# Norm factors spread from their two columns, lambda worked out in the first mixer, and a tail by groups in seven transfers

## The chip, the cores and the metric

One Trainium2 chip, one core of it. The metric is the device time of one execution in microseconds; the median of three runs stands for a kernel. Where a profile is read, it is one further execution taken by the hardware profiler, with its own time.

## The reference

One inference step of a two-layer diffusion backbone, for 128 context tokens and 128 latent tokens of width 2048, in float32. In short:

```
for l in range(2):
    mod = silu(cond) @ w_ada[l] + b_ada[l]          # six vectors: shift, scale, gate, twice
    h = rmsnorm(x, g_norm_mix[l]) * (1 + sc1) + sh1
    x = x + gt1 * (mixer_ab(h) if l == 0 else mixer_c(h))
    h = rmsnorm(x, g_norm_ffn[l]) * (1 + sc2) + sh2
    x = x + gt2 * conv_ffn(h)                       # up 2048 -> 2 x 5632, conv of 3, silu gate, down
y = rmsnorm(x, g_final)
rmsnorm(x, g) = x * rsqrt(mean(x * x) + EPS) * g    # over a token's 2048 features
mixer_c: softmax(q1 k1) - lam * softmax(q2 k2), then v, a norm per head, * (1 - lambda_init), w_out
         lam = exp(sum(lq1 * lk1)) - exp(sum(lq2 * lk2)) + lambda_init
```

The context tokens use their own condition vector and attend to themselves; the latent tokens attend to themselves and to 128 cached keys. `mixer_ab` has eight heads of latent attention and eight of grouped-query attention. The outputs are y of both groups and the new cache tensors.

## The kernel before, in words

**Layout.** Features stand on the 128 partitions, tokens on the free dimension: x is a tile of 16 chunks (`KD`) of 128 features by 256 tokens (`NT`), the context tokens first (`T` = 128 each). The tokens of the two requests are the two groups g = 0, 1, which have modulation vectors of their own.

**Products.** Each float32 product is made of three on split operands: a weight tile is loaded raw (1 MB), ACT rounds it to a high half `wh` (line 244), DVE subtracts to get the low half `wl` (line 245), and `gemm` (lines 330 to 348) multiplies wh by the operand's high and low halves and wl by its high half. A product of one output chunk is 16 steps k of three such matmuls. `between` hooks run inside the steps; where a hook is given, the order on TensorE is kept as written (`keep_order`).

**Order.** The program is recorded through a tile framework whose scheduler simulates the engines and puts the instructions of each engine in an order of its own; each engine then executes its list in order. `keep_order` pins instructions against each other, and `pe.in_turn` does so for TensorE in some stages. A change of one instruction can thus move many others in the stages that aren't pinned, the first mixer's heads above all. Work for adaLN (the product of silu(cond) with w_ada, 96 MB) is spread over all stages by rates: `pump` (line 568) is called after each product and does as many steps of it as its rate has made due; `side_pump` and `side_step` do the "side" blocks on DVE (lines 482 to 526, tiles `aacc`, `block`, `amside`), at the rates of `SIDE` (line 83), and `side_flush` does what is left at the end of a stage.

**Norms.** `stat_add` squares a finished chunk of x on ACT and POOL adds it to `sqacc`; the last square stays apart. `stat_rstd` (line 220) sums over the partitions with four matmuls of one column, DVE adds EPS (`rv`, line 208), POOL takes the power -1/2 (`rr`, line 211). The result is a column for each group: tokens on the partitions, one number each. `diagonal` (line 228) turns these into two 128x128 diagonal matrices on DVE, and `spread` (line 235) multiplies a matrix of ones with them, so that every partition holds the factors of all 256 tokens in PSUM. This is done at the start, for the latents and keys of the first mixer, at three entries, and at the end.

**Entries.** At the FFN of layer 0, the mixer of layer 1 and its FFN, `modulated` (line 673) hides the norm: the first three output chunks are multiplied with unnormalised rows `u` and scaled afterwards (`scaled`), while the normalised, modulated rows are made for the rest: `row` (line 735), sixteen times, on DVE (x by the factor, 737; low half, 749), ACT (743; cast, 747) and POOL (745, 749). The hooks stand in line 710: in chunk 0, step 8, the statistic and the diagonal (`stats`); in chunk 1, step 2, the spread (`factor`); line 713: in chunk 1, step 11, the first adaLN sums (`sums(0)`), which also start two loads. Line 720 copies the factors to SBUF on ACT.

**Layer 1's mixer** (`mixer_c`, line 1093) begins with lambda: a product of two columns on DVE, one matmul with ones, an exponential on ACT (line 1101), a combination on DVE (`nlam`). Then `project(h)` makes q, k and v of each of eight heads: the first head's first three products are the ready ones of `modulated`. `rope` (line 771) rotates q and k, four DVE operations each. `attend` follows in pieces between later products.

**Tail.** The last FFN's down projection ends with chunk 15: `residual` (line 761) on DVE, its square on ACT, `norm_scale`, a copy of the factors on ACT (line 1351), and then 16 chunks of the output: five (`EARLY`) that already carry g_final on POOL, eleven on DVE (line 1357), sent in five transfers by `SENT` (lines 58, 1359).

Of the kernel before, what the change touches and what calls it, by code (L numbers as in the profile page):

```python
# [12 lines left out]
AF = mybir.ActivationFunctionType  # L13
# [44 lines left out]
SENT = (4, 8, 12, 14, 16)  # L58
# [24 lines left out]
SIDE = {"in3": 0.6, "heads": 1.05, "out0": 0.9, "c": 1.7, "outc": 0.7}  # L83
# [5 lines left out]
def step_kernel(ctx: ExitStack, tc: tile.TileContext, A: dict):  # L89
# [138 lines left out]
    def diagonal(r, cols):  # L228
        dg = T_(tmp, [P, 2 * T], "diag", bufs=1)
        for i, c in enumerate(cols):  # L230
            dve.tensor_scalar(out=dg[:, i * T:(i + 1) * T], in0=ident, scalar1=r[:, c:c + 1],
                              scalar2=None, op0=ALU.mult)
        return dg

    def spread(dg, cols=(0, 1), bank=bank):

        ps = bank()
        n = len(cols) * T
        pe.matmul(ps[:, :n], ones, dg[:, :n], start=True, stop=True)
        return ps[:, :n]  # L240
# [354 lines left out]
    def norm_scale(st):  # L595
        return spread(diagonal(stat_rstd(st, D), (0, 1)))
# [76 lines left out]
    def modulated(st, l, which, W, u, to, rp):  # L673


        ensure(l, 3 * which + 1)
        ensure(l, 3 * which)
        while later:
            later.pop(0)()
        for q in range(4):  # L680
            raw_shift(u, l, which, q)
        if which:
            ada["i"] += len(BESIDE[l])
        unit = ROWS[ada["i"]]
        raws, got = [], {}

        def load_tile():
            raw = T_(wpool, [P, 4, 512], "araw", bufs=2)
            sp.dma_start(out=raw, in_=A["w_ada"][unit[0], unit[1], unit[2], len(raws)])
            raws.append(raw)  # L690

        def stats():
            got["r"] = stat_rstd(st, D, att_bank)
            got["dg"] = diagonal(got["r"], (0, 1))

        def factor():
            got["rb"] = spread(got["dg"], bank=att_bank)

        def sums(t):
            for i in range(2):  # L700
                sum_rows(t + i, raws[t + i])
            if t == 0:
                load_tile()
                load_tile()
            else:
                ada["i"] += 1
                steps.extend(ada_finish(*unit, False))
                steps.pop(0)()
# [11 lines left out]
        act.copy(rbs, rb)  # L720
# [12 lines left out]
        return hx, ready, [(lambda: steps.pop(0)(keep_order))] if steps else []  # L733
# [17 lines left out]
    def scaled(p, rb):  # L751
# [7 lines left out]
        return t  # L759

# [73 lines left out]
    def mixer_ab(hx, rb0, beside):  # L834
        l = 0
        with tc.tile_pool(name="ab", bufs=1) as ab:
            with tc.tile_pool(name="abp", bufs=1) as pj:
# [39 lines left out]
                def latents(c):  # L877
                    stat_add(sk, ck[:, c], 4)
                    if c == 3:
# [4 lines left out]
                        dg = diagonal(r, (0, 1))  # L884
                        yield
                        rb = spread(dg)
# [15 lines left out]
                def keys(c):  # L902
# [4 lines left out]
                    for g in range(2):  # L907
# [4 lines left out]
                    dg = diagonal(r, (0, 1))  # L912
                    yield
                    dve.scalar_tensor_tensor(out=kb[:, c], in0=kb[:, c], scalar=C("gkn"),
                                             in1=spread(dg), op0=ALU.mult, op1=ALU.mult)
# [84 lines left out]
            with tc.tile_pool(name="abh", bufs=1) as hp:  # L1000
# [33 lines left out]
                flush()  # L1034
                start(gqa_query(0))
# [57 lines left out]
    def mixer_c(cp, hx, W, ready, st):  # L1093
        l = 1
        lm = T_(cp, [P, 2], "lm")
# [4 lines left out]
        ex = T_(cp, [P, 2], "ex")  # L1100
        act.activation(ex, ps[:, 0:2], AF.Exp)
        nlam = T_(cp, [P, 1], "nlam")
        dve.scalar_tensor_tensor(out=nlam, in0=ex[:, 1:2], scalar=-LAMBDA_INIT, in1=ex[:, 0:1],
                                 op0=ALU.add, op1=ALU.subtract)

        xh, xl = (lambda k: hx[:, k, :NT]), (lambda k: hx[:, k, NT:2 * NT])
# [12 lines left out]
        def project(h):  # L1119
# [8 lines left out]
            if h == 1:  # L1128
                side_start("c", BESIDE[1], cp, True)
            for dst, to in ((q, T), (k, 2 * T)):  # L1130
# [5 lines left out]
                rope(dst[:, :, to:], ev[:, :, T:], 2, 64, "rch", "rsh")  # L1136
# [8 lines left out]
        def attend(h, q, k, v, evs):  # L1145
# [40 lines left out]
            for g in range(2):  # L1186
# [48 lines left out]
    def ffn(hx, W, ready, turn, l, st):  # L1235
# [4 lines left out]
        with tc.tile_pool(name=f"ffn{l}", bufs=1) as fp, banks(f"pffn{l}") as pf:  # L1240
# [41 lines left out]
            def down(gs, q):  # L1282
# [4 lines left out]
                for c in range(KD):  # L1287
# [5 lines left out]
                    residual(ps, l, 1, c, st if q == NQ - 1 else None)  # L1293
# [55 lines left out]
    rb = norm_scale(st)  # L1349
    rbs = T_(tmp, [P, NT], "nt", bufs=4)  # L1350
    act.copy(rbs, rb)
# [141 lines left out]
```

## Time and profile before

| | |
|---|---|
| median of 3 runs | 2343.69 us (2340.28 to 2348.35) |
| profiled execution | 2345.54 us |
| its span, first to last instruction | 2343.8 us |
| granted TensorE clock, mean | 0.995 |
| busy TensorE / DVE / ACT / POOL | 2296.9 / 1852.7 / 1193.2 / 182.3 us |
| moved by DMA | 612.97 MB, mean 262 GB/s |

How to read the rows: a row of time is start, duration, engine, line, operation, output <- input, sizes, and in brackets the idle time of the engine before it and what ended it. PE is TensorE's matmul, PEld its weight load; DVE is VectorE, ACT ScalarE, POOL GpSimd, SP the engine that issues the transfers. The list of waits has total time, number, longest. A row of windows has the stretch, its length, busy time (and count) of PE, PEld, DVE, ACT and POOL, then the granted TensorE clock as a share of full speed, the DMA share and GB/s. A row of the chain has start, duration, what. Lines are those of the kernel before. A float32 matmul outside the three-part products leaves two records, for two passes.

### The profile page before, as it was taken

What the parts mean: (1) busy time and instruction counts of PE and PEld (TensorE: products, weight loads), DVE (VectorE), ACT (ScalarE), POOL (GpSimd) and SP (SyncE); (2) the same over time, 40 slices, a digit from 0 to 9 for tenths busy, and PEclk for the clock granted to TensorE, in tenths of its full rate; (3) what the DMA queues carried; (4) which work ended last, traced back from release to release, by engine and by line L of the source; (5) the groups of instructions that cost most, each with busy time, mean ns of one, the idle gap of its engine ahead of it and who ended that gap; (6) DMA issues with size and microseconds to landing.
All of it is one profiled execution on the core that took longest, in us unless ns stands there. A gap on an engine that the chain in (4) does not pass through costs nothing.

```text
span 2343.8 us, 47878 instructions
## 1 busy us (share of the span) xinstructions
PE 2296.9 (98%) x19650; PEld 2186.5 (93%) x19650; DVE 1852.7 (79%) x2879; ACT 1193.2 (51%) x1979; POOL 182.3 (8%) x250
## 2 busy tenths in 40 slices
PE   6999999999999999999999999999999999999997
PEld 4789768999999999999989999999999999999997
DVE  3569767789999999999978888797899755666654
ACT  4245545565553355555564544456655434555543
POOL 0001201210000000001130000023000000000011
PEclk9999999999999999999999999999999999999999
DMA  9988888677767777777778888777677555555553
GB/s 369 357 324 294 300 326 328 236 278 270 261 247 298 292 268 258 266 269 253 288 261 279 299 308 313 242 278 251 253 261 265 195 198 195 190 192 197 198 190 117
DMA packets 106523, 612.97 MB, mean 262 GB/s; under 512 B 11520, under 2 KB 19392, under 8 KB 38592
## 3 DMA queue, kind: packets, MB, share of 16 engines
q1 hardware_dynamic: 106304, 609.92, 71.8%
q8 instruction: 154, 2.52, 0.4%
q14 instruction: 65, 0.53, 0.1%
HBM read 605.12 MB, written 4.75 MB: 260 GB/s over the span
## 4 chain that ended last, share of the span: by engine, by line
PE 92%; DVE 3%; DMA 2%; POOL 1%; ACT 1%; issue 1%; SPq 0%; DVEq 0%; POOLq 0%; ACTq 0%
PE acc L104 84%; PE ada L104 3%; PE att L104 2%; DVE wl L245 1%; POOL block L745 1%; PE att L107 1%; DMA raw<-w_in_ab 1%; DMA block<-w_ada 1%; PE misc L104 1%; DMA araw<-w_ada 0%; POOL hx L749 0%; ACT wh L244 0%; PE ada L107 0%; DVE aacc L488 0%; DVE block L737 0%
## 5 line engine op out<-in xcount | busy, mean ns | idle before, releaser
L244 ACT CAST wh<-raw 128x1024 fp32r<-128x1024 f32 (+2 forms) x824 | 795.1, 976 | 936.3 <-PE acc L104 755.7
L104 PE MATMUL acc<-hx,wh 128*128 128x256 f32 (+1 forms) x7296 | 1261.2, 278 | 5.9 <-ACT hx L621 4.3
L245 DVE TENSOR_TENSOR wl<-raw,wh 128x1024 fp32r<-128x1024 f32 (+2 forms) x824 | 918.7, 1130 | 301.5 <-ACT wh L244 294.8
L104 PEld LDWEIGHTS acc<-hx,wh 128*128 128x128 f32 x7296 | 1102.4, 188 | 35.1 <-issue 15.4
L104 PE MATMUL acc<-hx,wl 128*128 128x256 f32 (+1 forms) x3648 | 1010.5, 277 | 5.7 <-DVE wl L245 5.7
L104 PEld LDWEIGHTS acc<-hx,wl 128*128 128x128 f32 x3648 | 686.0, 188 | 10.8 <-DVE wl L245 7.3
L104 PE MATMUL acc<-g,wh 128*128 128x256 f32 x2816 | 478.9, 276 | 0.0
L104 PEld LDWEIGHTS acc<-g,wh 128*128 128x128 f32 x2816 | 423.9, 188 | 0.0
L104 PE MATMUL acc<-g,wl 128*128 128x256 f32 x1408 | 388.2, 276 | 0.0
L459 DVE CUSTOM_DVE_ANT_0 junk<-araw,condb 128x2048 f32<-128x2048 f32 x120 | 275.7, 2297 | 0.0
L104 PE MATMUL acc<-hxc,wh 128*128 128x256 f32 (+1 forms) x1536 | 269.3, 279 | 3.9 <-DVE hxc L749 3.9
L104 PEld LDWEIGHTS acc<-g,wl 128*128 128x128 f32 x1408 | 264.2, 188 | 0.0
L104 PEld LDWEIGHTS acc<-hxc,wh 128*128 128x128 f32 x1536 | 234.1, 189 | 4.7 <-DVE hxc L749 4.3
L104 PE MATMUL acc<-hxc,wl 128*128 128x256 f32 (+1 forms) x768 | 218.8, 285 | 0.0
L200 POOL TENSOR_TENSOR sqacc<-sqacc,sq 128x256 f32<-128x256 f32 x62 | 72.2, 1165 | 1508.2 <-ACT sq L196 1501.6
L488 DVE SCALAR_TENSOR_TENSOR aacc<-block,condw,aacc 128x512 f32<-128x512 f32 x240 | 171.8, 746 | 9.9 <-DMA block<-w_ada 9.7
L104 PEld LDWEIGHTS acc<-hxc,wl 128*128 128x128 f32 x768 | 145.6, 190 | 8.7 <-issue 5.4
L104 PE MATMUL ada<-araw,condw 128*32 128x512 f32 (+1 forms) x736 | 90.1, 589 | 12.6 <-DMA araw<-w_ada 12.6
L1251 ACT ACTIVATE cv<-acc,convw 128x256 f32<-128x256 f32 x170 | 94.9, 558 | 0.0
L764 DVE SCALAR_TENSOR_TENSOR x<-acc,mod,x 128x128 f32<-128x128 f32 x192 | 57.8, 342 | 41.4 <-PE acc L104 41.2
L1257 DVE SCALAR_TENSOR_TENSOR cv<-acc,convw,cv 128x254 f32<-128x254 f32 x170 | 81.3, 478 | 3.3
L1254 DVE SCALAR_TENSOR_TENSOR cv<-acc,convw,cv 128x254 f32<-128x254 f32 x170 | 80.6, 474 | 0.0
(224 smaller groups left out, 1407.1 us busy)
## 6 DMA issues: line engine op xcount, KB each, us to landing
raw<-w_up SPq DMA_DIRECT2D x176, 1024.0 KB, 4.8
araw<-w_ada SPq DMA_DIRECT2D x146, 1024.0 KB, 5.8
raw<-w_down SPq DMA_DIRECT2D x88, 1024.0 KB, 4.8
raw<-w_in_c SPq DMA_DIRECT2D x48, 1024.0 KB, 6.0
block<-w_ada SPq DMA_DIRECT2D x128, 256.0 KB, 5.4
raw<-w_in_ab SPq DMA_DIRECT2D x19, 1024.0 KB, 7.1
raw<-w_out_ab SPq DMA_DIRECT2D x16, 1024.0 KB, 8.3
raw<-w_out_c SPq DMA_DIRECT2D x16, 1024.0 KB, 5.4
```

Of the source, the lines that this page charges most:

```text
L104: return self.placed(nc.tensor.matmul(*a, **kw))
L107: return self.placed(nc.tensor.transpose(*a, **kw))
L200: eng.tensor_tensor(out=st["acc"], in0=st["acc"], in1=sq, op=ALU.add)
L244: pin(act.copy(out_hi, src))
L245: pin(dve.tensor_tensor(out=out_lo, in0=src, in1=out_hi.bitcast(F32), op=ALU.subtract))
L459: keep_order(dve.tensor_tensor_reduce(out=T_(feat["pool"], [P, D], "junk"), in1=feat["row"][:, c], in0=feat["raw"].rearrange("p g n -> p ( ...
L488: i = dve.scalar_tensor_tensor(out=acc[c], in0=block, scalar=condw[:, k, c:c + 1], in1=acc[c], op0=ALU.mult, op1=ALU.add)
L745: pool.tensor_scalar(out=h[:, s], in0=h[:, s], scalar1=a_, scalar2=b_, op0=ALU.mult, op1=ALU.add)
L764: dve.scalar_tensor_tensor(out=x[:, c, s], in0=ps[:, s], scalar=mod[:, l, 3 * which + 2, c, g:g + 1], in1=x[:, c, s], op0=ALU.mult, op1=AL ...
L1251: pin(act.activation(y, ps, AF.Identity, scale=cw[:, 1, m:m + 1], bias=cw[:, 3, m:m + 1]))
L1254: pin(dve.scalar_tensor_tensor(out=y3[:, :, 1:], in0=p3[:, :, :T - 1], scalar=cw[:, 0, m:m + 1], in1=y3[:, :, 1:], op0=ALU.mult, op1=ALU.add))
L1257: pin(dve.scalar_tensor_tensor(out=y3[:, :, :T - 1], in0=p3[:, :, 1:], scalar=cw[:, 2, m:m + 1], in1=y3[:, :, :T - 1], op0=ALU.mult, op1=A ...
```

## The change

- `diagonal` goes. `spread` takes the two columns of factors: for each group one matmul whose stationary operand is the column, repeated 128 times by its access pattern, and whose moving operand is the identity (128 columns).
- In `modulated` the statistic stands at step 6 of chunk 0 (was 8), the spread at step 13 of chunk 0 (was step 2 of chunk 1), the first adaLN sums at step 6 of chunk 1 (was 11).
- Lambda (`weigh_lambda`) is recorded in the first mixer, ahead of its heads; its result is kept.
- In the first head of layer 1, q's rotation is recorded behind k's copies.
- In the heads of layer 1 the factor 1 - lambda_init is folded into the constants of the variance: one POOL operation less per head.
- The rate of the side blocks in layer 1's output projection is 0.95 (was 0.7).
- The tail: the last chunk's residual and square go by groups (`last_residual`), each group's sum has a PSUM bank of its own and its own addition (`final_rstd`), DVE's first output chunk stands ahead of ACT's copy of the factors, and y is sent in seven transfers (1, 2, 3, 3, 3, 2, 2 chunks).

In the built program the scheduler moves instructions in 125 places of TensorE's list, most of them in the first mixer; q's rotation in the first head of layer 1 stands a little later on DVE than before, but still ahead of the last two even rows. The table load for exponentials, once in the first mixer and once in layer 1's mixer before, stands at lambda in the first mixer and at the first head's exponential in layer 1.

```diff
-SENT = (4, 8, 12, 14, 16)
+SENT = (1, 3, 6, 9, 12, 14, 16)
...
-SIDE = {"in3": 0.6, "heads": 1.05, "out0": 0.9, "c": 1.7, "outc": 0.7}
+SIDE = {"in3": 0.6, "heads": 1.05, "out0": 0.9, "c": 1.7, "outc": 0.95}
...
-    def diagonal(r, cols):
-        dg = T_(tmp, [P, 2 * T], "diag", bufs=1)
-        for i, c in enumerate(cols):
-            dve.tensor_scalar(out=dg[:, i * T:(i + 1) * T], in0=ident, scalar1=r[:, c:c + 1],
-                              scalar2=None, op0=ALU.mult)
-        return dg
-
-    def spread(dg, cols=(0, 1), bank=bank):
+    def spread(r, bank=bank):
 
         ps = bank()
-        n = len(cols) * T
-        pe.matmul(ps[:, :n], ones, dg[:, :n], start=True, stop=True)
-        return ps[:, :n]
+        for g in range(2):
+            pe.matmul(ps[:, g * T:(g + 1) * T], r[:, g:g + 1].to_broadcast([P, P]), ident, start=True, stop=True)
+        return ps[:, :NT]
...
         def stats():
             got["r"] = stat_rstd(st, D, att_bank)
-            got["dg"] = diagonal(got["r"], (0, 1))
 
         def factor():
-            got["rb"] = spread(got["dg"], bank=att_bank)
+            got["rb"] = spread(got["r"], bank=att_bank)
...
-        hooks, steps = [{8: stats}, {2: factor}, {}], []
+        hooks, steps = [{6: stats, 13: factor}, {}, {}], []
         load_tile()
         load_tile()
-        hooks[1][11] = lambda: sums(0)
+        hooks[1][6] = lambda: sums(0)
...
+    def last_residual(ps, l, which, c, st):
+        sq = T_(tmp, [P, NT], "sq", bufs=2)
+        for g in range(2):
+            s = slice(g * T, (g + 1) * T)
+            keep_order(dve.scalar_tensor_tensor(out=x[:, c, s], in0=ps[:, s],
+                                                scalar=mod[:, l, 3 * which + 2, c, g:g + 1],
+                                                in1=x[:, c, s], op0=ALU.mult, op1=ALU.add))
+            keep_order(act.activation(sq[:, s], x[:, c, s], AF.Square))
+        st["last"] = sq
+
+    def final_rstd(st):
+        cols = [bank(), T_(pacc, [P, 512], "acc")]
+        for src, start in ((st["acc"], True), (st["last"], False)):
+            for g in range(2):
+                keep_order(pe.matmul(cols[g][:, 0:1], src[:, g * T:(g + 1) * T], inv(D), start=start, stop=not start))
+        return rstd([c[:, 0:1] for c in cols], 2)
...
                 flush()
+                weigh_lambda()
                 start(gqa_query(0))
...
-    def mixer_c(cp, hx, W, ready, st):
-        l = 1
-        lm = T_(cp, [P, 2], "lm")
+    nlam = T_(keep, [P, 1], "nlam")
+
+    def weigh_lambda():
+        lm, ex = T_(small, [P, 2], "shift"), T_(small, [P, 2], "shift")
...
+            turned = []
             for dst, to in ((q, T), (k, 2 * T)):
...
-                rope(dst[:, :, to:], ev[:, :, T:], 2, 64, "rch", "rsh")
+                turned.append((dst[:, :, to:], ev[:, :, T:]))
+                while turned and not (quiet and dst is q):
+                    rope(*turned.pop(0), 2, 64, "rch", "rsh")
...
-            pool.tensor_scalar(out=var, in0=ss, scalar1=1.0 / 256, scalar2=EPS,
+            left = (1.0 - LAMBDA_INIT) ** 2
+            pool.tensor_scalar(out=var, in0=ss, scalar1=1.0 / (256 * left), scalar2=EPS / left,
                                op0=ALU.mult, op1=ALU.add)
             pool.tensor_tensor(out=var, in0=var, in1=C("mhalf")[:, 0:2], op=ALU.pow)
-            pool.tensor_scalar(out=var, in0=var, scalar1=1.0 - LAMBDA_INIT, scalar2=None,
-                               op0=ALU.mult)
...
-    rb = norm_scale(st)
+    rb = spread(final_rstd(st))
     rbs = T_(tmp, [P, NT], "nt", bufs=4)
-    act.copy(rbs, rb)
     sent = 0
     for c in range(KD):
...
+        if c == 0:
+            act.copy(rbs, rb)
```

More of the change, by code (lines that the diff above doesn't have):

```diff
@@ L595, in norm_scale @@
     def norm_scale(st):
-        return spread(diagonal(stat_rstd(st, D), (0, 1)))
+        return spread(stat_rstd(st, D))
     def modulate(hx, rb, l, which, chunks, fixed=False):
@@ L883, in latents @@
                         yield
-                        dg = diagonal(r, (0, 1))
                         yield
-                        rb = spread(dg)
+                        rb = spread(r)
                         for i in range(4):
@@ L911, in keys @@
                     yield
-                    dg = diagonal(r, (0, 1))
                     yield
                     dve.scalar_tensor_tensor(out=kb[:, c], in0=kb[:, c], scalar=C("gkn"),
-                                             in1=spread(dg), op0=ALU.mult, op1=ALU.mult)
+                                             in1=spread(r), op0=ALU.mult, op1=ALU.mult)
                     act.copy(kg[:, c, 0:T], kb[:, c, 0:T])
@@ L1099, in mixer_c @@
         keep_order(pe.matmul(ps[:, 0:2], ones, lm, start=True, stop=True))
-        ex = T_(cp, [P, 2], "ex")
         act.activation(ex, ps[:, 0:2], AF.Exp)
-        nlam = T_(cp, [P, 1], "nlam")
         dve.scalar_tensor_tensor(out=nlam, in0=ex[:, 1:2], scalar=-LAMBDA_INIT, in1=ex[:, 0:1],
                                  op0=ALU.add, op1=ALU.subtract)
+    def mixer_c(cp, hx, W, ready, st):
+        l = 1
         xh, xl = (lambda k: hx[:, k, :NT]), (lambda k: hx[:, k, NT:2 * NT])
@@ L1292, in down @@
                     ps = gemm(WD.chunk(), lambda k: gs[k][:, :NT], lambda k: gs[k][:, NT:2 * NT])
-                    residual(ps, l, 1, c, st if q == NQ - 1 else None)
+                    if l == NL - 1 and q == NQ - 1 and c == KD - 1:
+                        last_residual(ps, l, 1, c, st)
+                    else:
+                        residual(ps, l, 1, c, st if q == NQ - 1 else None)
                     if rows:
```

## The prediction

> **What bounds the kernel now.** I read the page's busy times first, then the list of who waited for whom with TensorE's own rows, then three places in time: the entry of layer 1, the first mixer, and the tail.
>
> ```profile
> span 2343.8 us, 47878 instructions
> PE 2296.9 (98%) x19650; PEld 2186.5 (93%) x19650; DVE 1852.7 (79%) x2879; ACT 1193.2 (51%) x1979; POOL 182.3 (8%) x250
> ```
> ```profile
> 520.00:1130.00 610.00, 610.00 (x5384) 610.00 (x5384) 567.63 (x719) 306.09 (x410) 10.03 (x7) 1.00 0.74 270
> ```
> ```profile
> PE acc L104 <- DVE wl L245: 5.7, 8, 2.1
> ...
> PE acc L104 <- DVE hxc L749: 3.9, 2, 2.6
> PE att L107 <- DVE p L821: 3.0, 3, 1.7
> ...
> PE misc L107 <- ACT amside L415: 0.8, 1, 0.8
> ```
> TensorE is the bound: it works in 2296.9 of 2343.8 us, and in the stretch from 520 to 1130 us (the first FFN) it never stands still. A step taken off another engine is worth nothing unless TensorE stands waiting for it. So the change can only earn what the second list holds (a few us in all) and the tail, where TensorE has nothing left to do. The other 99% of the span it cannot shorten.
>
> **The profiled execution and the median.** It took 2345.54 us (span 2343.8), 1.85 above the median 2343.69 of the three runs; I take the sum against its own stops and then subtract it from the median.
>
> **(a) The entry of layer 1.** In the two chunks ahead of the modulated operand TensorE multiplies raw rows, while DVE, ACT and POOL make the modulated rows `hxc`, which the fourth chunk reads in order.
>
> ```profile
> 1207.25 0.38 PE L104 MATMUL acc<-hxc,wh 128*128 128x256 f32 x1 [2.56 <-DVE hxc L749]
> 1209.59 0.58 PE L104 MATMUL acc<-hxc,wh 128*128 128x256 f32 x1 [1.38 <-DVE hxc L749]
> ```
> ```profile
> 1180.54 0.79 PE att L104 x8
> 1181.33 3.71 PE acc L104 x30
> 1185.03 0.45 PE att L104 x2
> 1185.48 1.40 issue
> ...
> 1201.43 0.48 DVE rope L779
> ...
> 1202.80 0.87 DVE dq L781
> ```
> ```profile
> 1185.56 0.37 ACT L720 COPY sq<-att 128x256 f32<-128x256 f32 x1 [0.31 <-PE att L104]
> ...
> 1201.78 1.28 ACT L1101 ACT_TABLE_LOAD   x1
> 1203.07 0.17 ACT L1101 ACTIVATE ex<-att 128x2 f32<-128x2 f32 x1
> ```
> ```profile
> 1185.50:1206.70 21.20, 19.18 (x159) 15.83 (x157) 18.12 (x40) 19.82 (x49) 17.98 (x23) 1.00 0.81 301
> ```
> TensorE stops twice, 2.56 + 1.38 = 3.94 us, for rows that come late. ACT is busy 19.82 of the 21.2 us in which they are made, DVE 18.12, POOL 17.98: all three are full, and none has a reserve. Two things leave this stretch. The spread moves from step 2 of the second chunk to step 13 of the first, five steps; 30 matmuls took 3.71 us, so a step of three takes 0.37 and the rows begin about 1.8 us earlier. Lambda's table load and exponential leave ACT, 1.28 + 0.17 = 1.45. Both together would be 3.25. But in the built order q's rotation (from 1201.43 on) still stands ahead of the last two even rows on DVE, and one 128x1024 subtraction as well: the deferral written in the kernel is mostly undone by the scheduler. So I don't grant the whole. I take 2.6 off; the ends are 1.0 (only part of the earlier start reaches the last row) and 3.94 (all stops gone; there is no more to gain).
>
> By the Trainium skill (ScalarE: Activation LUTs, What ACT_TABLE_LOAD costs) a switch of the set costs a load of about 1283 ns and then a drain, some 2.66 us in all. The load agrees with the row above; of a drain the rows show nothing, since the exponential starts 1.29 us after the load. No wait is seen ahead of the load either. By the page the part of (a) would be 1.2 us larger, and still be capped at 3.94.
>
> The load itself isn't saved: one stands ahead of head 0's first exponential instead. It has no wait of its own in the built program, and ACT stood idle there for POOL; I cost it at nothing, and at 1.28 on the head's chain if that cover is gone, which TensorE meets only at the transposes some chunks later.
>
> **(b) The first mixer.** Here the order of the instructions is made anew by the scheduler: 125 places on TensorE differ, nearly all here. What is computed is the same, less six half diagonals on DVE, and plus lambda's product, exponential and table load, which now stand early in the mixer. Today TensorE stops three times for a head's transposes, 3.0 us together, longest 1.7. In the order before, these late heads have the least TensorE work between scores and transposes; in the new order one of the three has about twice as much, and the others about as much as before. So I expect a little less of it: -0.7. Ends: -3.0 (all three gone) and +5.1 (three more of the longest), because a new order can also put a matmul ahead of its operand.
>
> **(c) The end of layer 1's output projection.** The rate of the side blocks goes from 0.7 to 0.95 a chunk, so the last unit's sums and transposes move from behind the last chunk into the chunks before it. The stop for `amside`, 0.8, goes; what would be late next is the last row's square, which stands behind that copy on ACT today and so comes earlier too. -0.8; ends -0.8 and 0.
>
> **(d) The two FFN entries.** The same early spread there, but rows already come in time; one stop each is left.
>
> ```profile
> 480.30 0.38 PE L104 MATMUL acc<-hx,wl 128*128 128x256 f32 x1 [0.62 <-DVE wl L245]
> ```
> ```profile
> 1632.13 0.38 PE L104 MATMUL acc<-hx,wl 128*128 128x256 f32 x1 [0.62 <-DVE wl L245]
> ```
> These wait for a weight's low half, which stands on DVE behind the last rows. With rows 1.8 us earlier they may vanish; a DVE queue ordered anew may also leave them. -0.6 of 1.24; ends -1.24 and 0. The earlier sums of the adaLN tile (step 6 instead of 11) are the same work in the same chunk: nothing.
>
> Does the spread now come too soon? Between statistic and spread TensorE has 7 steps, 7 x 0.37 = 2.6 us.
>
> ```profile
> 1181.76 1.08 POOL L211 TENSOR_TENSOR rr<-rv,cst 128x2 f32<-128x2 f32 x1 [8.58 <-DVE rv L208]
> ```
> The statistic ended at 1181.33 and POOL's power at 1181.76 + 1.08 = 1182.84, 1.5 us later, with DVE's addition between them. That leaves 1.1 of cover, and in the built order the addition stands ahead of the next subtractions, not behind one as before. Cost nothing; if a 1.3 us pair of subtractions slipped in front it would be some 0.2 for each of three entries.
>
> **(e) The spread itself.** Today one product of 256 columns, 0.45 us on TensorE in the row at 1185.03. Now two of 128 columns with a weight load each. The trace doesn't show it in this form; the statistic's eight passes of one column, 0.79, give 0.1 a pass, so four passes cost at least 0.4 and, with their columns, at most the 0.45 and two more such passes, 0.65. So 0 to +0.2 for each of six in the stream; I take +0.05 each, +0.3, since those passes are nearest to the ones at hand; ends 0 and +1.2. At the start of the program the spread stands behind a block of sums that ends after the diagonal, so nothing is gained there.
>
> **(f) The tail.**
>
> ```profile
> 2329.01 0.62 DVE x L764 x2
> ...
> 2329.72 0.42 ACT sq L196
> ...
> 2330.19 0.84 PE misc L104 x6
> ...
> 2331.05 0.17 DVE rv L208
> ...
> 2331.29 0.71 POOL rr L211
> ...
> 2332.03 0.49 DVE diag L231 x2
> ...
> 2332.66 1.21 PE misc L104 x2
> ...
> 2333.89 0.38 ACT nt L1351
> ```
> ```profile
> 2331.50:2332.00 0.50, 0.00 (x0) 0.00 (x0) 0.00 (x0) 0.00 (x0) 0.49 (x1) 1.00 0.00 0
> 2332.00:2332.50 0.50, 0.00 (x0) 0.00 (x0) 0.47 (x2) 0.00 (x0) 0.00 (x0) 0.69 0.00 0
> 2332.50:2333.00 0.50, 0.34 (x1) 0.37 (x2) 0.01 (x1) 0.00 (x0) 0.00 (x0) 0.50 0.00 0
> ...
> 2336.00:2336.50 0.50, 0.00 (x0) 0.00 (x0) 0.50 (x2) 0.00 (x0) 0.50 (x2) 0.50 0.12 49
> 2336.50:2337.00 0.50, 0.00 (x0) 0.00 (x0) 0.50 (x2) 0.00 (x0) 0.50 (x1) 0.50 0.99 401
> ...
> 2341.50:2342.00 0.50, 0.00 (x0) 0.00 (x0) 0.00 (x0) 0.00 (x0) 0.00 (x0) 0.50 0.46 176
> ```
> By groups: the second group's square begins when its half is ready, at 2329.7 as today, but is only half as long (0.3), and behind it stands one product instead of three; the sum for POOL is ready near 2330.6 instead of 2331.22, -0.6. The diagonal and its way to TensorE go, 2332.66 - 2332.03 = -0.6. The spread then starts near 2331.5. Its 1.21 us was at a granted clock of 0.50; at 2331.5 the clock still stood at 1.00, where the same spread took 0.45 in the stream: -0.5, if the clock holds. Behind the spread nothing is faster: DVE's first chunk goes ahead of ACT's copy, but the built program makes the copy wait for it and DVE's second chunk wait for the copy, so the same three follow each other. What then ends last is the transfer: it runs at 401 GB/s from 2336.5 to about 2341.75 without a gap, and 2.1 MB at that rate are 5.25 us, longer than DVE and POOL need to make them. So only an earlier start counts, and the first piece of one chunk fills 0.33 us before the others can follow: -0.3. Sum -2.0; I take -1.9. Ends -2.3 and -1.0 (clock at half, and small pieces at a lower rate).
>
> The Trainium skill (TensorE: Matmul & The Clock Gate, Part 1: The HAM clock gate) says that the clock falls to half after an idle window of about 3.4 us and that the window runs freely. The trace agrees: the last dense product ended at 2329.0 and the clock fell near 2332.2, 3.2 us later. By that rule the spread at 2331.5 runs at full clock in some executions and at half in others, 0.5 us apart.
>
> **The rest** (one POOL operation less for each head of layer 1, transfers, buffers): off TensorE's path, nothing.
>
> **Sum.** -2.6 - 0.7 - 0.8 - 0.6 + 0.3 - 1.9 = -6.3: 2339.2 against the profiled execution, 2337.4 against the median.
>
> **Rivals.**
> All stops go (chance 0.34): the rows are early enough, the clock holds, the mixer loses its stops. -3.94 - 2.0 - 0.8 - 1.24 + 0.2 - 2.1 = -9.9: 2333.8. For it speaks 3.25 of relief against 3.94 of stops; against it that ACT, DVE and POOL are all full there.
> The rows stay the bound (0.13): rotation and subtraction keep the last rows late, (a) gives 1.0, (d) nothing, the clock is at half: -1.0 - 0.7 - 0.8 + 0.3 - 1.4 = -3.6: 2340.1. This is also the case in which the deferral doesn't do what it says.
> The new order stops TensorE in the first mixer (0.09, slower): it executes in order, so each head's transposes that stand too soon behind their scores cost what the longest does now, 1.7 us. From four more such heads of sixteen on, the 5.6 that the rest earns is used up; with eight, 13.6 - 5.6 = +8: 2351.7. Against it: three of sixteen stop today, and in the new order the distances are not shorter on the whole.
>
> **How the numbers follow.** The forecast has 0.44, at 2337.4, its own range 2335 to 2340. About 0.3%, 7 us, can be told from no change. Faster than 2336.7: nearly all of the first rival and a small part of the forecast, 0.37. Slower than 2350.7: 0.07. Between: 0.56. The range reaches from 2332.4 (all best ends: -3.94 - 3.0 - 0.8 - 1.24 - 2.3 = -11.3) to 2343.2, where (b) is at its worst and the others as forecast (-6.3 + 0.7 + 5.1 = -0.5); most of the slower rival stays out.
>
> **What would show it.** (a) The stops for `hxc` in layer 1's entry fall from 3.9 to about 1.3 and ACT's first copy of the spread comes five steps earlier; (b) stops for `p` in the mixer near 2; (c) no stop for `amside`; (d) one of the two 0.62 stops left; (e) two products of 0.25 each in the stream; (f) no diagonal, a granted clock of 1.00 at the last spread, and transfers that start about 3 us earlier against the last product. Wrong would be: new waits of TensorE for weights or transposes in the mixer above 3 us, a wait for the power at a spread, or a gap in the last transfers above 1 us.

## The result, and the profile after

The changed kernel takes 2366.77 us (median of five runs, 2363.06 to 2368.09) against 2343.69 (2340.28 to 2348.35): a ratio of 1.0091, 95% interval 1.0073 to 1.0109 (all ratios below are to the kernel before, run beside the other on the same chip). It is slower by 17 to 26 us, where 6.3 less was forecast. Its profiled execution took 2368.09 us (span 2366.2).

First the head of the page and the waits of TensorE after the change (total, times, longest).

```profile
span 2366.2 us, 47897 instructions
...
PE 2324.9 (98%) x19666; PEld 2214.9 (94%) x19666; DVE 1852.1 (78%) x2864; ACT 1191.0 (50%) x1980; POOL 177.8 (8%) x242
```
```profile
PE acc L104 <- DVE wl L238: 4.7, 6, 2.6
...
PE ada L104 <- DMA araw<-w_ada: 3.1, 3, 2.3
...
PE misc L104 <- POOL rr L211: 1.0, 1, 1.0
...
PE att L107 <- DVE p L830: 0.3, 1, 0.3
...
PE acc L104 <- DVE hxc L741: 0.2, 1, 0.2
```
The stops that the change was to remove are gone: `hxc` 3.9 to 0.2, `p` 3.0 to 0.3, `diag` and `amside` no longer in the list. New are three for `araw` (3.1 together) and one for POOL's power `rr` in the tail (1.0, where `diag` stood with 1.6). TensorE stands still for 5.6 us less in all (span less busy time, 46.9 before and 41.3 after). Yet TensorE is busy 28.0 us longer, with 16 records more. So the time isn't in a wait. The views of two stretches, one in each FFN, in the kernel before (the second row; its first stands in the prediction) and after:

```profile
1720.00:2320.00 600.00, 600.00 (x5297) 600.00 (x5296) 405.33 (x533) 295.78 (x389) 15.75 (x13) 1.00 0.57 201
```
```profile
520.00:1130.00 610.00, 610.00 (x5385) 610.00 (x5384) 566.95 (x719) 306.55 (x410) 9.78 (x7) 1.00 0.74 269
1720.00:2320.00 600.00, 600.00 (x5096) 600.00 (x5096) 392.59 (x510) 281.88 (x367) 12.86 (x10) 1.00 0.56 197
```
In layer 0's FFN (FFN 0) the counts agree to one product. In layer 1's (FFN 1), TensorE is busy for every one of 600 us at a granted clock of 1.00 in both, and does 5096 products instead of 5297. The starts of the blocks of three products show how, in the kernel before and after:

```profile
1700.15 0.39 PE L104 MATMUL acc<-hx,wh 128*128 128x256 f32 x2
1700.49 0.39 PE L104 MATMUL acc<-hx,wh 128*128 128x256 f32 x2
...
1703.21 0.39 PE L104 MATMUL acc<-hx,wh 128*128 128x256 f32 x2
```
```profile
1700.05 0.40 PE L104 MATMUL acc<-hx,wh 128*128 128x256 f32 x2
1700.40 0.40 PE L104 MATMUL acc<-hx,wh 128*128 128x256 f32 x2
...
1703.23 0.40 PE L104 MATMUL acc<-hx,wh 128*128 128x256 f32 x2
```
From the first to the last row are nine blocks, 27 products: 3.06 us before, 113.3 ns each; 3.18 after, 117.8 each. It isn't a few late products; all of them are 4.45 ns further apart, in the up and in the down projection, to the last. This distance from the start of one product to the start of the next is called the cadence below. The weight loads show it too: in these 600 us the mean load of `wl` takes 192 ns after and 188 before, that of `wh` 188 in both. The row has 6070 products, from four transposes of an adaLN tile (`am`) in the third chunk that the FFN multiplies itself to the last product: 6070 x 4.45 ns = 27.0 us.

By stages, from the first product of each to the next (us):

| from | before | after | change |
|---|---|---|---|
| start to `kv_in` | 220.65 | 223.14 | +2.5 |
| first mixer, to the raw rows of FFN 0 | 230.22 | 232.31 | +2.1 |
| FFN 0's entry and first up part | 247.69 | 246.33 | -1.4 |
| the rest of FFN 0 | 478.88 | 478.88 | 0 |
| layer 1's entry and mixer, to its output projection | 323.19 | 318.93 | -4.3 |
| output projection | 102.35 | 101.87 | -0.5 |
| FFN 1's entry and first up part | 247.12 | 254.41 | +7.3 |
| the rest of FFN 1 | 478.88 | 497.66 | +18.8 |
| tail | 14.79 | 12.69 | -2.1 |

### The profile page after: what moved, and what is told of

The parts are those of the page before. It is cut to its first block, busy times and chain, and to the rows that moved or that the text cites. A ratio compares the mean times of both kernels' runs of the same rounds, so it can differ in the third digit from the quotient of the medians.

```text
span 2366.2 us, 47897 instructions
## 1 busy us (share of the span) xinstructions
PE 2324.9 (98%) x19666; PEld 2214.9 (94%) x19666; DVE 1852.1 (78%) x2864; ACT 1191.0 (50%) x1980; POOL 177.8 (8%) x242
## 4 chain that ended last, share of the span: by engine, by line
PE 95%; DVE 2%; DMA 2%; ACT 1%; issue 0%; POOL 0%; DVEq 0%; ACTq 0%
PE acc L104 87%; PE ada L104 4%; PE att L104 2%; DMA araw<-w_ada 1%; PE att L107 1%; DVE wl L238 1%; PE misc L104 0%; PE ada L107 0%; DMA raw<-w_in_ab 0%; DVE sqacc L200 0%; DVE x L1370 0%; DMA cst<-cst 0%; ACT wh L237 0%; DVE aacc L481 0%; DMA block<-w_ada 0%
## 5 line engine op out<-in xcount | busy, mean ns | idle before, releaser
L104 PE MATMUL acc<-hx,wh 128*128 128x256 f32 (+1 forms) x7296 | 1278.8, 280 | 6.6 <-ACT hx L614 4.3
L104 PE MATMUL acc<-g,wh 128*128 128x256 f32 x2816 | 488.2, 278 | 0.0
L104 PEld LDWEIGHTS acc<-hxc,wh 128*128 128x128 f32 x1536 | 233.3, 188 | 0.7 <-DVE hxc L741 0.4
```

Of the source, the lines that this page charges most:

```text
L104: return self.placed(nc.tensor.matmul(*a, **kw))
```

## The experiments

**The theory**: TensorE's row of such products has two cadences, 113.3 and 117.8 ns. Which one it takes is settled ("drawn") whenever other matmuls have come between, and is then kept until the next such place. Both stand in both kernels, in short rows of the mixers; in the long row of FFN 1 the changed kernel drew the slow one. A program draws alike each time as far as the times tell: every execution of the changed kernel lies at least 14 us above every one of the kernel before. **Rivals**: the new places of the tiles (lambda's number takes a slot of 32 bytes ahead of hx and the weights, and the diagonal's 1 KB goes) make every product slower; or the other engines hold TensorE up.

**1 and 2. The place of the last transposes.** Changed kernel, `ffn` of layer 1 alone; `gemm` calls hooks behind a named product of a block:
```
...
-            in_order = [{}, {}] + turn + [{}]
+            in_order = [{}, {}] + ([{(8, 0): t} for t in turn] if l else turn) + [{}]
```


> The changed kernel with one product of 256 columns moved: in the third chunk that layer 1's FFN multiplies itself, the four transposes of am stand behind the first product of block 8 instead of behind the second. Nothing else differs on any engine. Theory (two cadences): TensorE's long row of products goes on at whichever spacing sets in behind the last foreign matmuls, 113.3 or 117.8 ns, until something else stands between them. A shift of the transposes by one product draws the spacing anew: the 6070 products of layer 1's FFN then run at 113.3 or again at 117.8, so the whole is near 2340 (2366.8 less 6070 x 4.45 ns = 27.0) or unchanged near 2367, and nothing in between. Rival (where the tiles lie): addresses are as in the changed kernel, so 117.8 ns and 2367. Rival (the other engines hold TensorE up): their work is as it was, so 117.8 ns and 2367. Only 2340 tells them apart.

The second has (9, 1) in place of (8, 0).

> The changed kernel with the four transposes of am in layer 1's FFN one whole block (three products, 340.0 ns) later, behind the second product of block 9. Theory (two cadences): drawn anew or, if what decides is the place within the block of three, drawn as before: 2340 or 2367, nothing between. Both rivals (places of the tiles, other engines): 117.8 ns and 2367.

Measured: 2365.90 (ratio 1.0084, 1.0070 to 1.0098) and 2364.65 (1.0085, 1.0066 to 1.0104). The row stays slow in both; nothing is told apart.

**3. All places put back.** An unused tile of the diagonal's size in `stat_rstd`, and lambda's number in a spare column of the constants.
```
+        T_(tmp, [P, 2 * T], "diag", bufs=1)
...
-    nlam = T_(keep, [P, 1], "nlam")
...
+        nlam = held["nlam"] = cst[:, _AT["lam"][0] + 1:_AT["lam"][0] + 2]
```


> The changed kernel with its tiles put back: an unused tile of 1 KB stands where the diagonal's was, and lambda's number is kept in a column of the constants that is no longer needed, so that hx, wh, wl, raw, g, cv and condb lie at the addresses of the kernel before. The order on TensorE, ScalarE, POOL and SP is that of the changed kernel. Rival (where the tiles lie): 113.3 ns in layer 1's FFN and 2340. Theory (two cadences): the entry is the same, so 117.8 ns and 2367, unless a shift of a nanosecond or so upstream draws the other one.

Measured: 2335.45 us, ratio to the kernel before 0.9954 (0.9940 to 0.9967). The row runs at 113.3 ns (stretch, length, TensorE busy and count, granted clock, DMA share, GB/s):

```profile
1720.00:2320.00 600.00, 600.00 (x5297) 1.00 0.56 199
```
With the same order on TensorE this is 31 us faster than the changed kernel and faster than the kernel before; 27 of the 31 lie in FFN 1, the rest at the start and in the first mixer, whose times vary among kernels of the same order. So places matter. The starts of TensorE at the transposes, in the changed kernel and in this one:

```profile
1637.78 0.40 PE L104 MATMUL acc<-hx,wh 128*128 128x256 f32 x2
1638.01 0.60 PE L107 MATMUL misc<-cst,am 128*128 128x128 f32 x4
...
1638.57 0.40 PE L104 MATMUL acc<-hx,wh 128*128 128x256 f32 x2
...
1638.92 0.40 PE L104 MATMUL acc<-hx,wh 128*128 128x256 f32 x2
...
1639.28 0.40 PE L104 MATMUL acc<-hx,wh 128*128 128x256 f32 x2
```
```profile
1632.14 0.39 PE L104 MATMUL acc<-hx,wh 128*128 128x256 f32 x2
1632.37 0.60 PE L107 MATMUL misc<-cst,am 128*128 128x128 f32 x4
...
1632.93 0.40 PE L104 MATMUL acc<-hx,wh 128*128 128x256 f32 x2
...
1633.28 0.39 PE L104 MATMUL acc<-hx,wh 128*128 128x256 f32 x2
...
1633.63 0.39 PE L104 MATMUL acc<-hx,wh 128*128 128x256 f32 x2
```
In the trace's nanoseconds the two agree to 1 ns over the whole entry, up to the transposes: the first starts 119 ns behind the last product in the changed kernel, 115 here. Behind them both run at the slow cadence for four products; then this one goes over to 113.3, and the changed kernel never does. FFN 0 of the changed kernel, with the same tiles at the same addresses, has 115 and is fast. So an address doesn't slow every product; it goes with another draw. The delay of the first transpose goes with the slow draw in FFN 1 of all kernels here but pad_less and order_hlh (119 or 120 ns where slow, 115 where fast), but doesn't make it by itself: in FFN 0 of run 10 the first transpose starts 118 ns behind, and the row is fast.

**4. The tail alone**, on the kernel before (`last_residual`, `final_rstd`, the direct spread and `SENT`, as in the diff).

> The kernel before with the tail alone changed: the last residual and square by groups, one bank a group, the spread without a diagonal there, the first chunk ahead of the copy, seven transfers. All up to the last chunk of layer 1's FFN is the kernel before, so both FFNs should run at its 113.3 ns a product and this shows part (f) by itself. By the prediction -1.9 us (-2.3 to -1.0): 2341.8 against 2343.7. If the tail itself costs: above 2343.7. If layer 1's FFN runs at 117.8 ns here, though nothing ahead of it differs, the theory that its entry decides has failed.

Measured: 2343.18 us against 2345.32 of the kernel before on that chip, ratio 0.9991 (0.9982 to 1.0000): -2.1. From the last product to the end 12.72 us against 14.79. The row of FFN 1 has 5296 products in the same 600 us. With the new tail alone the trace gains what part (f) forecast.

**5 to 8. Which places.** `lambda_back` takes the second edit of run 3 alone, `diag_back` the first alone; `pad_less` shortens the pad ahead of the weights:
```
-    T_(wpool, [P, 48], "pad", bufs=1)
+    T_(wpool, [P, 40], "pad", bufs=1)
```
and `before_32` adds `T_(keep, [P, 1], "nlam")`, unused, to the kernel before.

> The changed kernel with lambda's number kept in a spare column of the constants: hx, wh, wl, raw, araw, am and sq are back at the addresses of the kernel before; nt, cv, g, condb and what follows lie 1024 bytes lower. The order of every engine is that of the changed kernel. Theory A (the 32 bytes under hx, wh, wl or am decide how the long row of products in layer 1's FFN settles): 113.3 ns a product there, 2335 to 2338. Theory B (the 1024 bytes under g and cv decide): 117.8 ns and 2362 to 2366. Theory C (places don't matter, and the fast row of the run with all places put back was chance): either.

> The changed kernel with an unused 1 KB tile where the diagonal's was: all tiles from sqacc on lie 32 bytes higher than in the kernel before, none 1024 lower. Orders of all engines as in the changed kernel. Theory A (32 bytes decide): 117.8 ns, 2362 to 2366. Theory B (1024 bytes decide): 113.3 ns, 2335 to 2338. Theory C: either.

> The changed kernel with the pad ahead of the weights 32 bytes shorter: raw, wh, wl, araw and am are back at the addresses of the kernel before, hx, sqacc and convw stay 32 bytes higher, nt, cv, g and condb lie 1024 lower. Orders of all engines as in the changed kernel. Theory A splits: if the weights or am carry the 32 bytes that matter, 113.3 ns and 2335 to 2338; if hx does, 117.8 and 2362 to 2366. Theory B: 117.8. Theory C: either.

> The kernel before with one unused tile of 4 bytes (a slot of 32) where the changed kernel keeps lambda's number: all tiles from sqacc on lie 32 bytes higher, orders of all engines as in the kernel before. Theory A (32 bytes decide, whatever the change did to the order): one of the long rows of products may settle at 117.8 ns, above all that of layer 1's FFN: 2371 against 2344.5. Theory that the new order and the 32 bytes decide together: 113.3 ns in both and 2344.5.

Measured: lambda_back 2336.06 (0.9962, 0.9948 to 0.9975), diag_back 2368.15 (1.0085, 1.0062 to 1.0108), before_32 2345.97 (1.0003, 0.9993 to 1.0013). With the new order the 32 bytes bring the slow row and the 1024 don't; with the old order the 32 bytes do nothing. pad_less is a case of its own: 2385.12 (1.0163, 1.0143 to 1.0183), and its FFN 0, fast in all other kernels, alternates (up, down, up, down; FFN 1 does the same):

```profile
500.00:700.00 200.00, 200.00 (x1693) 1.00 0.68 245
720.00:820.00 100.00, 100.00 (x885) 1.00 0.78 293
850.00:1050.00 200.00, 200.00 (x1693) 1.00 0.68 250
1090.00:1190.00 100.00, 100.00 (x884) 1.00 0.74 271
```
Here the up parts take 118.1 ns a product (200/1693) and the down parts 113.0, with uneven spacings of 115 to 124 ns in the up parts. In the built program hx begins at byte 28288, a multiple of 64, and the weights at 104096, 32 past one; g, the down parts' operand, lies 32 past one like the weights. The trace's other stages agree: the products of hx take 118.3 ns on average in each long stretch of them, also in the first mixer and the output projection, while those of hxc, which lies like the weights, take 114.7, about as in lambda_back (114.9). In all other kernels operand and weights agree in this. In this case that is a rule of place, and it isn't what the changed kernel suffers from.

**9. Other matmuls in the middle of the slow row.** The changed kernel with four more transposes, never read:
```
-            in_order = [{}, {}] + turn + [{}]
+            def again():
+                pt = bank()
+                for b in range(4):
+                    keep_order(pe.transpose(pt[:, b * P:(b + 1) * P], ident, ident))
+
+            in_order = [{}, {}] + turn + [{}] + ([None] * 8 + [again] if l else [])
```


> The changed kernel with four more transposes (of the identity, 128 columns each, never read) in the twelfth chunk that layer 1's FFN multiplies itself, and nothing else changed on any engine. Theory (two cadences, kept until foreign matmuls come between): the row runs at 117.8 ns up to them and may go on at 113.3 from there, since in the other runs four such transposes have left the slow cadence for the fast one in 16 of 19 places. Some 5640 of the 6070 products stand behind: 2366.8 - 5640 x 4.44 ns (25.0) + 4 x 0.11 + 0.2 = 2342 to 2343. If they leave it as it was: 2367.4. Rival (places of the tiles hold the whole row at 117.8): 2367.4.

Measured: 2341.75 us, ratio 0.9984 (0.9974 to 0.9993). Before and behind the four transposes at 1695.45:

```profile
1650.00:1690.00 40.00, 40.00 (x342) 1.00 0.65 237
1700.00:1740.00 40.00, 40.00 (x356) 1.00 0.72 262
```
The same row, with the same tiles at the same places and the same orders on all other engines, goes at 117.0 ns ahead of them (40/342) and at 112.4 behind (40/356; two or three products at the borders of a window are counted too many, and the trace's nanoseconds give 117.9 and 113.3). Less than a microsecond of useless work earns 25. That shows the cause of the 27 us: the cadence is a state of the row, which other matmuls in it can change. Both rivals fall.

**10. The place of `am`.** A pad of 32 bytes ahead of am, sq and nt, taken off again behind them.

> The changed kernel with a pad of 32 bytes ahead of am, sq and nt, taken off again behind them: am, sq, nt and the small tiles lie 32 bytes higher, hx, wh, wl, raw, g, cv and condb where the changed kernel has them. The trace of the changed kernel leaves that of the run with all places put back (34 us alike to 1 ns) at the first transpose of am, which starts 5 ns later. Theory (am's place makes that delay): 115 ns ahead of the first transpose, 113.3 in the row, near 2340. Rival (the delay comes from the weights or hx at their new place, or from other traffic): 119 ns, 117.8 and 2366.

Measured: 2364.93 (1.0079, 1.0062 to 1.0095), slow. It isn't am's own place.

**11. The spread put back**, on lambda_back:
```
-        hooks, steps = [{6: stats, 13: factor}, {}, {}], []
+        hooks, steps = [{8: stats}, {2: factor}, {}], []
-        hooks[1][6] = lambda: sums(0)
+        hooks[1][11] = lambda: sums(0)
```


> The run with lambda's number in the constants (2336.1), with the statistic and the spread of the three later norms put back to where the kernel before had them: statistic in step 8 of the first chunk, spread in step 2 of the second, sums in step 11. By the prediction's account of (a) the rows then come 1.8 us later and TensorE stops up to 1.8 us for hxc, plus 0.6 for (d): 2337.9 to 2338.5. If the earlier spread was worth nothing, 2336.1. If it takes back all of what layer 1's entry gained (stops for hxc 3.9 to 0.2): 2339.8. A row of 6070 products at 117.8 ns, 27.0 us more, would be drawn anew and is to be read apart.

Measured: 2346.02 us, ratio 1.0011 (0.9986 to 1.0036). More than any of the three numbers: the stops for hxc come back (3.5 us), and half the granted clock behind them. Against lambda_back the trace is 5.5 us longer in layer 1's entry and mixer and 1.0 in each FFN's entry (start and first mixer differ by +4.4 and -3.9, within what they vary by). The windows at the stops:

```profile
1208.00:1210.00 2.00, 1.60 (x6) 0.73 0.92 273
1210.00:1212.00 2.00, 0.81 (x3) 0.50 0.95 363
1212.00:1214.00 2.00, 2.00 (x11) 0.50 0.75 254
1214.00:1216.00 2.00, 2.00 (x12) 0.56 0.82 154
1216.00:1218.00 2.00, 2.00 (x20) 1.00 0.60 246
```
Eleven or twelve records in 2 us where a window at full clock has 20. One of this kernel's ten executions took 2372.81, 27 above the median: as much as one long row at the other cadence, but there is no trace of it.

**12 and 15. Lambda put back to layer 1's entry**, on lambda_back: `weigh_lambda()` is called at the head of `mixer_c` instead of in the first mixer; in the second run with `lm` and `ex` in the mixer's pool.

> The run with lambda's number in the constants (2336.1), with lambda's product, exponential and table load put back to the entry of layer 1; the spread stays early. By the prediction's account of (a) ACT then has 1.45 us more ahead of the last rows, so stops for hxc of up to 1.45: 2336.1 to 2337.6. If lambda alone made the entry late: 2339.8. If it stood beside other work: 2336.1, with no stop for hxc. The first mixer's order is made anew too: the stops for araw there (3.1 us in the changed kernel) go if lambda's place caused them.

> The run with lambda's number in the constants (2336.1), with lambda's product, exponential and table load put back to layer 1's entry and its small tiles kept in the mixer's pool as in the kernel before; the spread stays early. By the prediction's account of (a): stops for hxc of up to 1.45 and 2336.1 to 2337.6. If lambda's load is what made the rows late: stops of 3 us and more, and the half clock behind them, 2341 to 2343. If it stood beside other work: no stop for hxc and 2336.

Measured: lambda_late 2343.67 (0.9992, 0.9982 to 1.0001), with a new stop of 3.8 us of lambda's own matmul for its product on DVE, so it says nothing on the question. lambda_cc, without that stop, 2338.72 and 0.9962 (0.9949 to 0.9975), the very ratio of lambda_back; stops for hxc 0.4. The first mixer's order differs between the two, but the stage in question is alike: layer 1's entry and mixer take 319.1 us in lambda_cc and 319.0 in lambda_back. Lambda's move is worth nothing that can be measured.

**13 and 14.** `shift_64` gives lambda's number 16 columns, a slot of 64 bytes; `order_hlh` exchanges the second and third product of each block.

> The changed kernel with a slot of 64 bytes instead of 32 for lambda's number: hx, wh, wl, raw, am 64 bytes higher than in the kernel before, nt, cv, g, condb 960 lower, so all lie within their 64 bytes as in the kernel before. Orders of all engines as in the changed kernel. If the place within 64 bytes decides what the row draws: 113.3 ns in layer 1's FFN, 2335 to 2340. If any new place can draw the slow cadence: 117.8 and 2365 is as open as 2338.

> The changed kernel with the three products of each block in the order wh-hi, wl-hi, wh-lo instead of wh-hi, wh-lo, wl-hi (one product is taken with the same operands in another place; the sum is the same). If the second cadence comes from two products with the same weights in a row: no row at 117.8 ns any more, 113.3 or one new value everywhere, and about 2335 less some 4 us of slow rows in the mixer. If it belongs to rows of such products whatever their order: both spacings again, 2338 or 2366 by what the FFNs draw.

Measured: shift_64 2363.69 (1.0066, 1.0049 to 1.0082), slow: the place within 64 bytes doesn't decide. order_hlh 2341.05 (0.9975, 0.9964 to 0.9987): both FFNs fast, but both cadences are there, in two rows of its second mixer:

```profile
1219.00:1235.00 16.00, 16.00 (x139) 1.00 0.76 246
1306.00:1322.00 16.00, 16.00 (x141) 1.00 0.83 283
```
(In the trace's nanoseconds 117.8 and 113.3; the counts also hold a few other matmuls.) So they don't come from two products with the same weights in a row.

**What stays open**: what delays the first transpose by 4 to 5 ns in FFN 1 of the new order once hx and the weights are shifted, whether that is what decides, and what the two states of the row are. The draws for FFN 1: old order, old places and +32: fast; new order, old places (old_places and lambda_back): fast; new order, shifted by 32 or 64 (six kernels): slow; the same shift with the products of a block exchanged (order_hlh): fast.

## Why the prediction was wrong

**The step that failed** is in the first part: "The other 99% of the span it cannot shorten", and with it "The rest (... transfers, buffers): off TensorE's path, nothing." A TensorE that never stands still was taken to have one speed. Here it has two at the same granted clock, and the change moved 6070 products to the other, +27.0 us. No rival had it; the slower one was a new stop in the first mixer.

**(a) Entry of layer 1**, -2.6: the stage gives -4.3. The stops fell to 0.2, nearly the end of 3.94, and what the sum left out is the half clock that the stops brought. The kernel before, at the stops:

```profile
1206.00:1208.00 2.00, 0.75 (x6) 1.00 1.02 356
1208.00:1210.00 2.00, 0.62 (x4) 0.80 1.00 420
1210.00:1212.00 2.00, 2.00 (x11) 0.50 0.68 240
1212.00:1214.00 2.00, 2.00 (x17) 0.84 0.31 94
```
It lasts 3.4 us, worth at most 1.7 (its first 0.4 us lie in the second stop). Stops and half clock make more than the 4.3; what took the rest back was not looked for. The account of (a) was wrong in its parts: 1.8 for the spread and 1.45 for lambda. Run 11 shows the earlier hooks to carry all of it, and run lambda_cc lambda's move nothing; why 1.8 us of earlier rows takes away more than 3 us of stops was not tried.

**(b) First mixer**, -0.7: the stops for `p` went, as hoped, but a stop for `araw` came, outside what was named:

```profile
289.61 1.08 PE L104 MATMUL ada<-araw,condw 128*32 128x512 f32 x4 [2.29 <-DMA araw<-w_ada]
```
The granted clock stood at 0.50 from 289.4 us on for 3.4 us besides. This stage took 229.1 to 230.2 us in three traces with the order before and 229.1 to 233.3 in eleven with the new one: between nothing and +3, within the ends (-3.0, +5.1), on the other side of the value.

**(c)** -0.8: the stop for `amside` went; the stage gives -0.5, and 0 in run 1, which has the same order there. Inside its ends (-0.8 and 0).

**(d), (e)** -0.6 and +0.3: both stops of 0.62 went, and the spread costs 0.02 more than before (from the product ahead of it to the second behind it 0.79 us before, 0.81 after). The two entries give -1.4 and, in lambda_back, where FFN 1 is fast, -0.9, and run 11, with the late hooks, takes back 1.0 in each. Mis-sized, on the right side: more than the best end of (d), -1.24.

**(f) Tail**, -1.9: -2.1. The clock held, and the spread went at 1.00 (last row, of windows):

```profile
2354.01 0.51 ACT L760 ACTIVATE sq<-x 128x128 f32<-128x128 f32 x2 [7.10 <-DVE x L757]
...
2355.25 0.70 POOL L211 TENSOR_TENSOR rr<-rv,cst 128x2 f32<-128x2 f32 x1 [7.47 <-DVE rv L208]
2356.00 0.71 PE L104 MATMUL misc<-cst,rr 128*128 128x128 f32 x4 [1.03 <-POOL rr L211]
...
2357.26 5.20 SPq L1375 DMA_DIRECT2D o_y<-x  x7
```
```profile
2356.00:2356.50 0.50, 0.50 (x4) 0.50 (x4) 0.00 (x0) 0.00 (x0) 0.00 (x0) 1.00 0.00 0
```
That the clock held was luck; the prediction had priced the other case at 0.5 us. Of fifteen traces with this tail, in six the clock fell before the spread had ended, and their tails are about 0.5 us longer. In run 10, for one, the spread took 1.22 us:

```profile
2353.73 1.22 PE L104 MATMUL misc<-cst,rr 128*128 128x128 f32 x4 [1.03 <-POOL rr L212]
```
```profile
2353.50:2354.00 0.50, 0.27 (x1) 0.28 (x2) 0.00 (x0) 0.00 (x0) 0.17 (x1) 0.50 0.00 0
2354.00:2354.50 0.50, 0.50 (x3) 0.50 (x4) 0.00 (x0) 0.00 (x0) 0.00 (x0) 0.50 0.00 0
```
**The start**, +2.5 up to `kv_in`, isn't the change's as far as the traces tell: kernels with the new order reach `ql`, a little ahead of it, between 212.4 and 217.5 us, and the kernel before at 213.4. The time goes with the half clock in the first 100 us: 3.4 us of it in the earliest of these, 13.7 in the latest.

Without the row of FFN 1 the total came out near: lambda_back, all of the change but with hx and the weights where they were, runs at 0.9962, 8.9 us below the kernel before (5.9 to 12.2), where 6.3 was predicted; that is near the first rival (all stops go, -9.9). In part that is luck: by the stages of its trace and that of the kernel before, layer 1's entry and mixer gave 4.3, the two FFN entries 2.3, the tail 2.1 and the start 1.4, and the first mixer took 3.0 back, so that terms too small and one on the wrong side made up for each other. The cover of 1.1 us between statistic and spread held: POOL's power ends a wait of TensorE only in the tail.

## What to carry to other kernels

Where an engine is busy without a stop, count its instructions in equal windows before and after: the count, not the busy share, shows its speed. Here a long uninterrupted row of matmuls kept the cadence with which it began, and a small change ahead of it together with one of the tiles' addresses moved the time by more than all the waits it removed; repeat such a change with the tiles' addresses held fixed before judging it. Ending a stop can also give back a half clock behind it, as in layer 1's entry.

## What the runs showed of the hardware

Products of 256 columns, three to a block with a weight load each, run at 113.3 or 117.8 ns for hundreds of us, at a granted clock of 1.00 in both. The Trainium skill (TensorE: Matmul & The Clock Gate, Back-to-back issue gap) gives one gap for a size, 262 cycles for 256 columns for an isolated product, and says that in a stream the spacing is set by matmul and weight load together; neither cadence is that figure (109 ns, an estimate from it at the 2.4 GHz that the same place names), and the choice between the two isn't described there. After some kinds of interruption the draw came out alike each time: in six traces (before, after, runs 1 to 4), where at least 20 products stand on either side, a fast row went on slow in all 31 cases after 16 sums from the adaLN tile `araw`, and fast in all 18 after 8 of them (after 8 from the tile `raw` in 15 of 22). And an operand that lay 32 bytes off its weights modulo 64 cost 118 ns a product in pad_less.

The half clock came after stops of 2.56 and 1.38 us with a short product between, and within a stop of 2.29 us (granted 0.50 from 289.4 us for 3.4 us). The Trainium skill (TensorE: Matmul & The Clock Gate, HAM oscillation — how this bites in real kernels) puts the limit at idle gaps of about 3.4 us; here shorter ones were enough, and the measurement decides.
